# Four parts of the modulation rows as running sums on VectorE, started beside the retention heads

## The chip, the cores and the metric

One core of one Trainium2 chip runs the whole kernel in one launch. The metric is the device time of a run in microseconds. The engines of the core each follow a queue of their own, in order: TensorE (PE, with its weight loads PEld), VectorE (DVE), ScalarE (ACT), GpSimd (POOL) and SyncE (SP), which issues most loads. They meet through semaphores only.

## What is computed

Two transformer blocks on 512 tokens of width 1024, with 256 tokens of context. Each block begins with a modulation, whose six rows of 1024 numbers scale, shift and gate the block's two branches:

```python
def _modulation(cvec, w, b, n):
    m = jax.nn.silu(cvec) @ w[:, : n * D_MODEL] + b[: n * D_MODEL]
    return jnp.split(m, n, axis=-1)

sh1, sc1, g1, sh2, sc2, g2 = [m[:, None, :] for m in _modulation(c, w_mod[i], b_mod[i], 6)]
cm = _modulation(c_ctx, w_mod[i], b_mod[i], 2 if last else 6)
...
hx = _rmsnorm(x, norm_mix_pre[i]) * (1.0 + sc1) + sh1
...
x = x + g1 * _rmsnorm(_mixer_out(ret_x, gdn_x, rg, gz, gates, *out_p), norm_mix_post[i])
h2 = _rmsnorm(x, norm_ffn_pre[i]) * (1.0 + sc2) + sh2
x = x + g2 * _rmsnorm(_moe(h2, *moe_p), norm_ffn_post[i])
```

A vector of 1024 goes through a matrix of 1024 x 6144 float32 numbers (25 MB), once in each block (`w_mod`, `w_mod_2`). The first two rows (`sh1`, `sc1`) are needed for the context vector too. The first block mixes by a gated delta net (gdn) and by retention, two heads of each in either direction, then runs a mixture of 64 experts; the second block mixes by a convolution and neighbourhood attention and runs 16 experts. The outputs of both mixers go through `w_gdn_out` and `w_ret_out`, then `w_o`.

## The kernel before

A modulation is computed in three parts of 2048 columns (`bk` 0 to 2, two rows each). Part 0 of `w_mod` comes first, before anything else can run; five parts are later ones. `mod_part` (lines 300 to 322) loads eight tiles of 128 x 2048 (1 MB each), one ahead of use, and multiplies each by the 32-column tile `cm` of the activated vectors, in four products that stand side by side in the array's four groups of 32 columns:

```python
for g in range(4):
    nc.tensor.matmul(ps[32 * g:32 * g + 32, :], cm[:, k, :], wt[:, g * 512:(g + 1) * 512],
                     start=(k == 0), stop=(k == ND - 1), tile_position=(0, 32 * g))
for _ in range(pause):
    yield
```

Then ScalarE copies the sums to `brow` (line 313), PE transposes them (line 228), and VectorE adds the bias into `mcol` (line 321). `mod_part` is a generator: `self.start` puts it on the list `chains`, and `tick`, which `dense` calls after every few products (line 253), moves each generator on by one `yield`. So ticks decide where between the large products the later parts are recorded, and that is the order of every engine's queue.

Before, `later_mods` starts at the head of the first mixer. It lays out the constants of retention (`ret_consts`), then the five parts with a pause of two ticks per tile, so all five lie beside the gdn heads, from 59 to 308 us of the span.

All tiles of large matrices (`w_mod`, `w_in`, `w_gdn_out`, `w_ret_out`, `w_o`, later the experts) come out of one pool of `NW` = 4 buffers, through `wload` (line 176) on SyncE's queue, in the order in which they are recorded. A load waits until a buffer's last reader is done. In most weights each tile is split into a high and a low half: a cast on ScalarE (line 211) and a subtraction on POOL or VectorE (line 212), and the product is three products of halves (line 253).

`mix_out` (lines 1140 to 1171) holds four buffers at once, two of `w_gdn_out` and two of `w_ret_out`. It takes the gdn side first (`br` = 1), then the retention side (`br` = 0), and before that side's splits it empties the list of generators:

```python
raw = [[self.wrows(n, 256 * i, 2) for i in range(2)] for n in ("w_gdn_out", "w_ret_out")]
for br in (1, 0):
    if br == 0:
        self.rows1 = self.mix_rows()
    while self.yT[br][0] is None or self.yT[br][1] is None or (br == 0 and self.chains):
        self.tick()
```

`mix_rows` needs rows of `w_mod`; the rows of `w_mod_2` are needed only in the second block.

Of the kernel before, what the change touches and what calls it, by code (L numbers as in the profile page):

```python
# [16 lines left out]
OP = mybir.AluOpType  # L17
# [4 lines left out]
P = 128  # L22
D = 1024
ND = 8
# [74 lines left out]
AHEAD, EARLY = 2, (2, 2, 3, 3)  # L99
W1, W2, W4, W5 = 5.5, 1.8, 6.0, 3.0  # L100
TAPS = 16

LOADS2, ORDER2 = 12, "vvvvbb"

# [14 lines left out]
class K:  # L119
# [180 lines left out]
    def mod_part(self, w, b, cm, mcol, bk, pause):  # L300
# [19 lines left out]
        for r in range(2):  # L320
            nc.vector.tensor_add(dst[:, :, :, r], pt.rearrange("p j (g q) -> p g j q", g=4)[:, :, :, r],
                                 self.bcol[:, 48 * b + 16 * bk:48 * b + 16 * bk + 16].rearrange("p (g j) -> p g j", g=4))

    def bcast_row(self, cols, name):

        nc = self.nc
        dst = self.u(D, name=name)
        for h in range(2):
            ps = self.ps(4, P)
            self.transposes(ps, [cols[:, 4 * h + k:4 * h + k + 1].to_broadcast([P, P]) for k in range(4)])  # L330
            nc.scalar.copy(dst[:, h * 512:(h + 1) * 512], ps.rearrange("p a b -> p (a b)"))
        return dst
# [77 lines left out]
    def phase_a(self):  # L410
        nc, a, cp = self.nc, self.a, self.cp
        self.setup()
        self.w_in1()
        xt = [self.u(D, name="xt") for _ in range(4)]
        ct = [self.u(D, name="ct") for _ in range(2)]
        for t in range(2):
            nc.scalar.dma_start(ct[t], a["ctx"][t * P:(t + 1) * P])
        for t in range(4):
            nc.scalar.dma_start(xt[t], a["x"][t * P:(t + 1) * P])
        cm = self.silu_cols(R_C, "1")  # L420
        mcol = self.mcol = cp.tile([P, 48, 2], F32, name="mcol1")
        hc, hx = [], []
        self.start(self.rows_T(ct, hc, "hc", 5), self.rows_T(xt, hx, "hx", 4))
        for i, _ in enumerate(self.mod_part("w_mod", 0, cm, mcol, 0, 3)):
            if i in (10, 11):
                self.w_fetch(i - 10)
            if i in (22, 23):
                for _ in self.w_split(i - 22, 0):
                    pass
            self.tick()  # L430
        self.drain()
        gm = self.col[:, R_GMIX:R_GMIX + 8]
        Ax = self.mod_cols(gm, mcol, 1, 0, "x1")
        Ac = self.mod_cols(gm, mcol, 1, 1, "c1")
        self.hx = self.split_T(hx, 2, Ax, mcol[:, 0:8, 0], "hx", nc.vector)
        self.hc = self.split_T(hc, 4, Ac, mcol[:, 0:8, 1], "hc", nc.gpsimd)
        del hx, hc
        self.ghalf = cp.tile([P, 8], F32, name="ghalf")
        nc.vector.tensor_scalar(self.ghalf, self.col[:, R_RGN:R_RGN + 8], 0.5, None, op0=OP.mult)
        self.yT = [[None, None], [None, None]]  # L440
        self.gsp = self.dp.tile([16, P, NX], F32, name="gsp")
        self.start(self.later_mods(cm))
        self.gates_ab()
        gs = [SimpleNamespace(p=p, k=0, v=0, q=0, z=[]) for p in range(2)]
        for g in gs:
            self.gdn_feats(g)
            self.start(self.gdn_chain(g))
            for i in range(8):
                self.gate_spill(8 * g.p + i)
            self.out_gate(g)  # L450
        rs = [SimpleNamespace(p=p, z=[]) for p in range(2)]
        for r in rs:
            self.ret_feats(r)
            self.start(self.ret_chain(r))
            self.out_gate(r)
        self.mT = self.mix_out()

    def later_mods(self, cm):
        nc = self.nc
        yield from self.ret_consts()  # L460
        for bk in (1, 2):
            yield from self.mod_part("w_mod", 0, cm, self.mcol, bk, 2)
        cm2 = self.silu_cols(R_C2, "2")
        mcol = self.mcol2 = self.cp.tile([P, 48, 2], F32, name="mcol2")
        for bk in range(3):
            yield from self.mod_part("w_mod_2", 1, cm2, mcol, bk, 2)

    def w_stream(self, name, tiles, ahead):

# [1393 lines left out]
    def phase_c(self):  # L1863
# [3 lines left out]
        ys, taps = self.conv_mixer(h)  # L1867
        qkv, rest = self.attn_proj(h, itertools.islice(taps, TAPS))
        self.attention(qkv, rest, itertools.chain(taps, self.conv_tail(ys)))
# [529 lines left out]
```

## Times and profile before

| | |
|---|---|
| runs shown | 2811.13, 2811.26 and 2801.1 us, median 2811.13 |
| the profiled run's own time | 2811.13 us |
| its span | 2809.2 us |
| granted clock of TensorE, mean | 0.954 |
| PE busy | 2486.5 us, 89% |
| VectorE, ScalarE, POOL busy | 1056.1, 515.1, 541.5 us |

The span runs from the first to the last profiled instruction, and the run's own time is 1.9 us longer. Busy time is a sum over stages: in the gdn stage (59 to 308 us) TensorE is hardly ever idle, and in the second half of the kernel the loads of experts run nearly without pause. A row of the timeline gives start, duration, line, operation, tiles, count, and in brackets the idle time ahead with what ended it.

### The profile page before, as it was taken

How to read it: one execution, taken by the hardware profiler on the slowest of the kernel's cores; microseconds unless marked ns; L12 is line 12 of the kernel's file. 1: busy time of each engine (PE TensorE's matmuls, PEld its weight loads, DVE VectorE, ACT ScalarE, POOL GpSimd, SP SyncE). 2: the span in 40 equal slices, each digit the busy share in tenths (PEclk: the TensorE clock that was granted, in tenths of full speed). 3: DMA queues.
4: the chain of work that ended last, by engine and by line, in shares of the span. 5: the costliest groups of instructions: out<-in, count | busy, mean ns of one | idle time of the engine just before them, and what ended most of it. 6: DMA issues, size and time to landing. Idle time of an engine off the chain costs nothing.

```text
span 2809.2 us, 34992 instructions
## 1 busy us (share of the span) xinstructions
PE 2486.5 (89%) x13409; PEld 1373.5 (49%) x13409; DVE 1056.1 (38%) x2675; ACT 515.1 (18%) x1088; POOL 541.5 (19%) x392
## 2 busy tenths in 40 slices
PE   6999989999799998987895969968999899988887
PEld 3767869887454543433344857533333333333322
DVE  3573763454733532222323777231211212112213
ACT  4442532222211110100112225110000000000001
POOL 3152243334312221222233450000000000000000
PEclk8999999999899999999897989989999999999999
DMA  7576221134479999999996122259999999999996
GB/s 266 215 271 217 94 87 46 61 117 158 158 256 336 337 335 346 345 346 319 329 330 210 32 79 81 117 242 422 426 427 426 427 427 427 427 427 426 427 427 291
DMA packets 160154, 782.13 MB, mean 278 GB/s; under 512 B 20787, under 2 KB 66035, under 8 KB 121075
## 3 DMA queue, kind: packets, MB, share of 16 engines
q1 hardware_dynamic: 131504, 714.65, 65.2%
q0 software_dynamic: 16288, 37.79, 5.7%
q10 hardware_dynamic: 12194, 27.45, 2.7%
q8 instruction: 107, 1.75, 0.3%
q14 instruction: 61, 0.49, 0.1%
HBM read 752.73 MB, written 33.23 MB: 280 GB/s over the span
## 4 chain that ended last, share of the span: by engine, by line
PE 67%; DMA 17%; DVE 11%; issue 2%; ACT 2%; POOL 2%; SPq 0%; DVEq 0%; ACTq 0%; POOLq 0%
PE ps L253 17%; PE ps L2265 13%; PE ps L2284 8%; DMA wu<-in_w_expert 6%; PE ps L1638 6%; DMA w<-in_w_expert 6%; PE ps L228 5%; PE ps L224 4%; DMA wd<-in_w_expert 3%; PE ps L2213 2%; PE ps L2296 2%; PE ps L1635 2%; PE ps L309 2%; POOL wsl L212 1%; PE ps L1668 1%
## 5 line engine op out<-in xcount | busy, mean ns | idle before, releaser
L2265 PE MATMUL ps<-w,xT 128*64 128x512 f32 x2048 | 444.8, 593 | 7.5 <-DMA w<-in_w_expert 5.9
L2265 PEld LDWEIGHTS ps<-w,xT 128*64 128x64 f32 x2048 | 146.8, 137 | 302.9 <-issue 277.2
L2284 PE MATMUL ps<-w,hT 128*64 128x512 f32 x1024 | 229.6, 607 | 18.7 <-ACT hT L2276 18.7
L212 POOL TENSOR_TENSOR wsl<-w,wsh 128x1024 fp32r<-128x1024 f32 x60 | 174.5, 2917 | 259.8 <-ACT wsh L211 193.8
L2320 POOL TENSOR_TENSOR fin<-fin,norm_final_g 128x512 f32<-128x512 f32 x2 | 2.6, 1306 | 1105.1 <-ACT fin L2313 1105.1
L2271 DVE TENSOR_TENSOR hid<-hid,ps 128x512 f32<-128x512 f32 x32 | 22.0, 687 | 405.7 <-PE ps L2265 405.7
L1638 PE MATMUL ps<-w,xT 128*128 128x512 f32 (+6 forms) x320 | 149.5, 610 | 19.3 <-DMA w<-in_w_expert 11.4
L224 PE MATMUL ps<-wd,ehT 128*128 128x512 f32 (+6 forms) x320 | 150.8, 615 | 15.5 <-DVE eh L1649 12.4
L2284 PEld LDWEIGHTS ps<-w,hT 128*64 128x64 f32 x1024 | 73.3, 140 | 166.4 <-issue 141.5
L1638 PE MATMUL ps<-wu,xT 128*128 128x512 f32 (+6 forms) x320 | 147.2, 599 | 2.0 <-DMA wu<-in_w_expert 2.0
L1604 POOL DMA_INDIRECT xg<-h2d,sidx x65 | 67.0, 1031 | 329.5 <-PE ps L1668 169.0
L1659 DVE COPY ehT<-ps 128x256 f32<-128x256 f32 (+6 forms) x69 | 22.8, 330 | 277.0 <-PE ps L228 277.0
L1648 ACT ACTIVATE eh<-ps 128x256 f32<-128x256 f32 (+6 forms) x69 | 23.2, 337 | 497.6 <-PE ps L1638 313.7
L2270 ACT ACTIVATE hid<-ps 128x512 f32<-128x512 f32 x32 | 19.1, 597 | 512.3 <-PE ps L2265 512.3
L2289 DVE TENSOR_TENSOR y<-ps,G 128x512 f32<-128x512 f32 x16 | 11.1, 691 | 268.3 <-PE ps L2284 268.3
L1638 PEld LDWEIGHTS ps<-w,xT 128*128 128x128 f32 (+6 forms) x320 | 52.8, 169 | 107.1 <-issue 98.1
L1901 DVE SCALAR_TENSOR_TENSOR cy<-cv,cw,cy 128x512 f32<-128x512 f32 x120 | 101.6, 904 | 0.4
L253 PE MATMUL ps<-hxh,wsh 128*128 128x512 f32 x296 | 88.6, 428 | 5.5 <-ACT wsh L211 3.1
L224 PEld LDWEIGHTS ps<-wd,ehT 128*128 128x128 f32 (+6 forms) x320 | 51.5, 171 | 85.0 <-issue 57.2
L1638 PEld LDWEIGHTS ps<-wu,xT 128*128 128x128 f32 (+6 forms) x320 | 50.2, 165 | 73.3 <-issue 67.8
L2299 DVE TENSOR_TENSOR xr<-xr,ps 128x512 f32<-128x512 f32 x128 | 78.1, 680 | 19.4 <-PE ps L2296 19.4
L253 PE MATMUL ps<-hxh,wsl 128*128 128x512 f32 x296 | 83.9, 416 | 0.0
(644 smaller groups left out, 4166.0 us busy)
## 6 DMA issues: line engine op xcount, KB each, us to landing
w<-in_w_expert SPq DMA_DIRECT2D x191, 2048.0 KB, 17.5
w<-in_w_expert SPq DMA_DIRECT2D x64, 1024.0 KB, 15.6
wu<-in_w_expert SPq DMA_DIRECT2D x128, 512.0 KB, 15.8
wd<-in_w_expert SPq DMA_DIRECT2D x128, 512.0 KB, 13.8
w<-in_w_mod SPq DMA_DIRECT2D x48, 1024.0 KB, 5.6
w<-in_w_in SPq DMA_DIRECT2D x34, 1024.0 KB, 5.6
wa<-in_w_in SPq DMA_DIRECT2D x9, 512.0 KB, 9.6
gsp<-gsp POOLq DMA_DIRECT2D x16, 256.0 KB, 3.0
```

What stands on the lines that cost most here:

```text
L212: (lo or self.nc.vector).tensor_sub(low, x, hi.bitcast(F32))
L224: self.nc.tensor.matmul(ps, l, r, start=(i == 0), stop=(i == n - 1))
L228: self.nc.tensor.transpose(ps[:, i], s, self.ident[:parts, :parts])
L253: self.nc.tensor.matmul(ps, l, r, start=(i == 0), stop=(i == n - 1))
L309: nc.tensor.matmul(ps[32 * g:32 * g + 32, :], cm[:, k, :], wt[:, g * 512:(g + 1) * 512], start=(k == 0), stop=(k == ND - 1), tile_position ...
L1604: self.nc.gpsimd.indirect_dma_start(out=self.xg[b % 4][:c], out_offset=None, in_=self.h2d, in_offset=bass.IndirectOffsetOnAxis(ap=idx[:c], ...
L1635: nc.tensor.matmul(ps[64 * j:64 * j + 64, 0:256], x, w[k][:, 256 * j:256 * j + 256], start=first, stop=last, tile_position=(0, 64 * j))
L1638: nc.tensor.matmul(ps[:m], x, w[k], start=first, stop=last)
L1901: nc.vector.scalar_tensor_tensor(y[:, j], vs[j][:, k:k + NX], tap, y[:, j], op0=OP.mult, op1=OP.add)
L2265: nc.tensor.matmul(pgu[gi][c][64 * j:64 * j + 64], xT[:, k], w[2 * j + c], start=(k == 0), stop=(k == ND - 1), tile_position=(0, 64 * j))
L2284: nc.tensor.matmul(py[64 * j:64 * j + 64], hT[fc][:, ff, 64 * fj:64 * fj + 64], w[2 * r + j], start=(ft == 0), stop=(ft == 15), tile_posit ...
L2299: nc.vector.tensor_add(xh, xh, ps)
```

## The change

A new method `mod_row` computes a part for the first vector alone, with VectorE in place of the large products. Two running sums `macc` of 128 x 1024 take tile after tile: the first is a multiplication by a column of `cm` (line 336 after the change), the other seven a multiplication and addition in one instruction (line 338). After the eighth tile four products with a tile of ones (line 343) sum over the 128 partitions, and copy, transposes and one addition follow as before. The pause is `MODS` = 3 ticks after each half tile. Parts 1 and 2 of both matrices go this way; part 0 of `w_mod_2` stays with `mod_part`, comes last, and pauses six ticks per tile.

`later_mods` starts after the loop over the gdn heads, and the constants of retention, until now its first step, start by themselves where it stood. Lines after the new method move by 32, those before it by 1.

```diff
--- before.py
+++ after.py
@@ -99,6 +99,7 @@
 AHEAD, EARLY = 2, (2, 2, 3, 3)
 W1, W2, W4, W5 = 5.5, 1.8, 6.0, 3.0
 TAPS = 16
+MODS = 3

 LOADS2, ORDER2 = 12, "vvvvbb"

@@ -320,6 +321,37 @@
         for r in range(2):
             nc.vector.tensor_add(dst[:, :, :, r], pt.rearrange("p j (g q) -> p g j q", g=4)[:, :, :, r],
                                  self.bcol[:, 48 * b + 16 * bk:48 * b + 16 * bk + 16].rearrange("p (g j) -> p g j", g=4))
+
+    def mod_row(self, w, b, cm, mcol, bk, pause):
+
+
+        nc = self.nc
+        load = lambda k: self.wload(self.a[w][k * P:(k + 1) * P, bk * 2048:(bk + 1) * 2048])
+        acc, nxt = [self.u(D, name="macc") for _ in range(2)], load(0)
+        for k in range(ND):
+            wt, nxt = nxt, load(k + 1) if k + 1 < ND else None
+            for h in range(2):
+                v = wt[:, h * D:(h + 1) * D]
+                if k == 0:
+                    nc.vector.tensor_scalar(acc[h], v, cm[:, k, 0:1], None, op0=OP.mult)
+                else:
+                    nc.vector.scalar_tensor_tensor(acc[h], v, cm[:, k, 0:1], acc[h], op0=OP.mult, op1=OP.add)
+                for _ in range(pause):
+                    yield
+        ps, brow = self.ps(), self.u(512, name="brow")
+        for g in range(4):
+            nc.tensor.matmul(ps[32 * g:32 * g + 32], self.ones[:, 0:32], acc[g // 2][:, g % 2 * 512:g % 2 * 512 + 512],
+                             start=True, stop=True, tile_position=(0, 32 * g))
+        yield
+        nc.scalar.copy(brow, ps)
+        yield
+        yield
+        pt = self.ps(4, P)
+        self.transposes(pt, [brow[:, j * P:(j + 1) * P] for j in range(4)])
+        yield
+        dst = mcol.rearrange("p (b g j) r -> p b g j r", b=3, g=4)[:, bk, :, :, 0]
+        nc.vector.tensor_add(dst, pt.rearrange("p j (g q) -> p g j q", g=4)[:, :, :, 0],
+                             self.bcol[:, 48 * b + 16 * bk:48 * b + 16 * bk + 16].rearrange("p (g j) -> p g j", g=4))

     def bcast_row(self, cols, name):

@@ -439,7 +471,7 @@
         nc.vector.tensor_scalar(self.ghalf, self.col[:, R_RGN:R_RGN + 8], 0.5, None, op0=OP.mult)
         self.yT = [[None, None], [None, None]]
         self.gsp = self.dp.tile([16, P, NX], F32, name="gsp")
-        self.start(self.later_mods(cm))
+        self.start(self.ret_consts())
         self.gates_ab()
         gs = [SimpleNamespace(p=p, k=0, v=0, q=0, z=[]) for p in range(2)]
         for g in gs:
@@ -448,6 +480,7 @@
             for i in range(8):
                 self.gate_spill(8 * g.p + i)
             self.out_gate(g)
+        self.start(self.later_mods(cm))
         rs = [SimpleNamespace(p=p, z=[]) for p in range(2)]
         for r in rs:
             self.ret_feats(r)
@@ -456,14 +489,13 @@
         self.mT = self.mix_out()

     def later_mods(self, cm):
-        nc = self.nc
-        yield from self.ret_consts()
         for bk in (1, 2):
-            yield from self.mod_part("w_mod", 0, cm, self.mcol, bk, 2)
+            yield from self.mod_row("w_mod", 0, cm, self.mcol, bk, MODS)
         cm2 = self.silu_cols(R_C2, "2")
         mcol = self.mcol2 = self.cp.tile([P, 48, 2], F32, name="mcol2")
-        for bk in range(3):
-            yield from self.mod_part("w_mod_2", 1, cm2, mcol, bk, 2)
+        for bk in (1, 2):
+            yield from self.mod_row("w_mod_2", 1, cm2, mcol, bk, MODS)
+        yield from self.mod_part("w_mod_2", 1, cm2, mcol, 0, 2 * MODS)

     def w_stream(self, name, tiles, ahead):

```

What this does to three queues at the place where the two sides of `mix_out` meet follows.

SyncE's queue issues the loads. Before, two loads of `w_in` and the mixers' output matrices stand ahead of the four loads of `w_o`:

```order
L176 DMA w_5375<-in_w_in 128x8x256
L176 DMA w_5621<-in_w_in 128x8x256
L176 DMA w_5889<-in_w_gdn_out 128x2x1024
L176 DMA w_5891<-in_w_gdn_out 128x2x1024
L176 DMA w_5893<-in_w_ret_out 128x2x1024
L176 DMA w_5895<-in_w_ret_out 128x2x1024
L176 DMA w_6301<-in_w_o 128x2x1024
L176 DMA w_6303<-in_w_o 128x2x1024
L176 DMA w_6305<-in_w_o 128x2x1024
L176 DMA w_6307<-in_w_o 128x2x1024
```

After, the series of loads that follows `w_gdn_out` is:

```order
L177 DMA w_5662<-in_w_gdn_out 128x2x1024
L177 DMA w_5664<-in_w_gdn_out 128x2x1024
L177 DMA w_5666<-in_w_ret_out 128x2x1024
L177 DMA w_5668<-in_w_ret_out 128x2x1024
L177 DMA w_5718<-in_w_mod 128x2048
L177 DMA w_5783<-in_w_mod 128x2048
L177 DMA w_6023<-in_w_mod 128x2048
L177 DMA w_6025<-in_w_mod 128x2048
L177 DMA w_6072<-in_w_mod 128x2048
L177 DMA w_6076<-in_w_mod 128x2048
L177 DMA w_6080<-in_w_mod 128x2048
L177 DMA w_6084<-in_w_mod 128x2048
```

The two loads `w_5718` and `w_5783` are the last of `w_mod`; behind them stand 24 loads of `w_mod_2`, then `w_o`, then the experts. Before, all 40 later loads of the modulation stand between loads of `w_in`, far ahead of this place.

On VectorE before, the retention head's last steps (`ro`, `yT`) are followed by the splits of the retention side (`yml`) and the gated sum of its first product (`gt`):

```order
L205 SCALAR_TENSOR_TENSOR rs_6175<-rqc_6185,rs_6175 128x8
L1136 TENSOR_SCALAR ro_5829<-ro_5829,bmv_6144,rs_6175 128x128 x8
L880 SCALAR_TENSOR_TENSOR yT_6217<-ps_6218,ghalf,gz_5764 128x512
L880 SCALAR_TENSOR_TENSOR yT_6217<-ps_6241,ghalf,gz_5764 128x512
L212 TENSOR_TENSOR yml_1284_6261<-yT_5636,ymh_1283_6260 128x1024
L212 TENSOR_TENSOR yml_1290_6273<-yT_6217,ymh_1289_6272 128x1024
L1163 SCALAR_TENSOR_TENSOR gt_6284<-gt_6284,ps_6286 128x512
```

After, behind the new column sums `cm` for the second block, the running sums stand between and behind them (`w_6023` is the first tile of `w_mod_2`):

```order
L297 TENSOR_TENSOR cm_1243_6013<-col,sce_6015 128x8x2
L392 SCALAR_TENSOR_TENSOR Af_6036<-mcol_106,col 128x8
L336 TENSOR_SCALAR macc_6021<-w_6023,cm_1243_6013 128x1024
L912 SCALAR_TENSOR_TENSOR yT_6028<-ps_6029,ghalf,gz_5532 128x512
L338 SCALAR_TENSOR_TENSOR macc_6021<-w_6025,cm_1243_6013,macc_6021 128x1024
L912 SCALAR_TENSOR_TENSOR yT_6028<-ps_6052,ghalf,gz_5532 128x512
L336 TENSOR_SCALAR macc_6022<-w_6023,cm_1243_6013 128x1024
L338 SCALAR_TENSOR_TENSOR macc_6022<-w_6025,cm_1243_6013,macc_6022 128x1024
L338 SCALAR_TENSOR_TENSOR macc_6021<-w_6072,cm_1243_6013,macc_6021 128x1024
L338 SCALAR_TENSOR_TENSOR macc_6022<-w_6072,cm_1243_6013,macc_6022 128x1024
L338 SCALAR_TENSOR_TENSOR macc_6021<-w_6076,cm_1243_6013,macc_6021 128x1024
```

All of part 1 and part 2 of `w_mod_2`, 32 instructions, stand there, ahead of the first gated sum.

On PE before, the transposes of the last rows stand directly ahead of the retention side's products (`ymh`, `wmh`):

```order
L228 MATMUL ps_6234<-cst,Af_6225 128x128 x4
L228 MATMUL ps_6218<-cst,ro_5829 128x128 x3
L228 MATMUL ps_6241<-cst,ro_5829 128x128
L228 MATMUL ps_6247<-cst,mcol_106 128x128 x4
L228 MATMUL ps_6253<-cst,mcol_106 128x128 x4
L228 MATMUL ps_6241<-cst,ro_5829 128x128 x3
L253 MATMUL ps_6286<-ymh_1283_6260,wmh_1285_6264 128x512
L253 MATMUL ps_6311<-ymh_1283_6260,wmh_1285_6264 128x512
L253 MATMUL ps_6332<-ymh_1283_6260,wmh_1285_6264 128x512
```

After, the end of part 2 of `w_mod_2` and the whole of its part 0 stand ahead of the first of those products:

```order
L343 MATMUL ps_6145<-macc_6112,cst 32x512 x2
L229 MATMUL ps_6152<-cst,brow_6146 128x128 x4
L310 MATMUL ps_6159<-w_6160,cm_1243_6013 32x512 x4
L310 MATMUL ps_6159<-w_6162,cm_1243_6013 32x512 x4
L310 MATMUL ps_6159<-w_6168,cm_1243_6013 32x512 x4
L310 MATMUL ps_6159<-w_6174,cm_1243_6013 32x512 x4
L310 MATMUL ps_6159<-w_6180,cm_1243_6013 32x512 x4
L310 MATMUL ps_6159<-w_6186,cm_1243_6013 32x512 x4
L310 MATMUL ps_6159<-w_6192,cm_1243_6013 32x512 x4
L310 MATMUL ps_6159<-w_6198,cm_1243_6013 32x512 x4
L229 MATMUL ps_6209<-cst,brow_6158 128x128 x4
L254 MATMUL ps_6242<-ymh_1291_6216,wmh_1293_6220 128x512
```

Eight groups of four products (line 310), each on a tile that is loaded there, have moved from the gdn stage to this place.

## Rows read from the trace of the kernel before

**Rows 1.** The page, part 1: engine, busy us (share of the span), instructions.

```profile
PE 2486.5 (89%) x13409; PEld 1373.5 (49%) x13409; DVE 1056.1 (38%) x2675; ACT 515.1 (18%) x1088; POOL 541.5 (19%) x392
```

**Rows 2.** PE by line and form: name, shape, count, busy us, mean ns.

```profile
L309 PE MATMUL ps<-w,cm 128*32 128x512 f32 x384 | 59.5, 631 | 2.8 <-DVE cm L296 2.4 <-DMA w<-in_w_mod 0.4
```

**Rows 3.** Windows of line 309 alone: stretch, PE busy (count), weight loads, clock, DMA, GB/s.

```profile
59.00:158.50 99.50, 20.79 (x128) 3.24 (x128) 0.97 0.60 212
...
158.50:203.00 44.50, 10.35 (x72) 1.65 (x72) 1.00 0.77 266
...
203.00:308.00 105.00, 18.13 (x124) 2.62 (x120) 1.00 0.61 209
```

**Rows 4.** Timeline of POOL near 73 us: start, duration, line, operation.

```profile
72.72 2.40 POOL L388 TENSOR_TENSOR hcl<-hc,hch 128x1024 fp32r<-128x1024 f32 x1
```

**Rows 5.** Timeline of PE near 77 and near 203 us.

```profile
77.00 0.63 PE L253 MATMUL ps<-hcl,wsh 128*128 128x256 f32 x4
...
203.00 0.31 PE L944 MATMUL ps<-Tc,Lc 32*32 32x32 f32 x8
```

**Rows 6.** Windows, all engines (PE, weight loads, DVE, ACT, POOL; clock, DMA, GB/s).

```profile
98.33:122.87 24.54, 24.02 (x159) 16.36 (x158) 22.00 (x77) 11.55 (x41) 3.97 (x2) 1.00 0.51 181
...
158.50:201.10 42.60, 42.60 (x229) 27.74 (x228) 39.41 (x96) 12.81 (x26) 11.92 (x13) 1.00 0.80 276
...
203.00:308.00 105.00, 105.00 (x917) 76.37 (x914) 40.11 (x129) 38.53 (x101) 31.68 (x34) 1.00 0.61 209
...
500.00:600.00 100.00, 95.75 (x670) 89.64 (x669) 48.39 (x155) 26.30 (x43) 37.96 (x21) 0.97 0.27 96
```

**Rows 7.** Timeline of DVE, end of the first inverse.

```profile
196.84 2.28 DVE L919 STREAM_TRANSPOSE Tc<-T 128x1024 f32<-128x1024 f32 x1
```

**Rows 8.** DVE by line and form, a multiplication and addition on 128x1024.

```profile
L1464 DVE SCALAR_TENSOR_TENSOR mix<-xr,rs,Ar 128x1024 f32<-128x1024 f32 x2 | 2.5, 1272 | 0.0
```

**Rows 9.** Timelines of POOL and DVE near 562 us.

```profile
562.31 2.81 POOL L212 TENSOR_TENSOR wml<-w,wmh 128x1024 fp32r<-128x1024 f32 x1 [11.90 <-ACT wmh L211]
...
559.19 0.29 DVE L1084 TENSOR_SCALAR vw<-rVc,rw 128x128 f32<-128x128 f32 x1 [0.70 <-ACT rVc L1060]
...
562.79 2.82 DVE L1084 TENSOR_SCALAR vw<-rVc,rw 128x128 f32<-128x128 f32 x3
```

**Rows 10.** Timelines of DVE and PE, end of the last retention head, output products.

```profile
628.45 0.75 DVE L880 SCALAR_TENSOR_TENSOR yT<-ps,ghalf,gz 128x512 f32<-128x512 f32 x1 [0.26 <-PE ps L228]
...
630.76 7.41 PE L253 MATMUL ps<-ymh,wmh 128*128 128x512 f32 x25 [2.34 <-ACT wmh L211]
...
659.81 5.49 PE L253 MATMUL ps<-wqh,mph 128*128 128x512 f32 x23
```

**Rows 11.** The page, part 6: loads, count, KB, median us from issue to landing.

```profile
w<-in_w_mod SPq DMA_DIRECT2D x48, 1024.0 KB, 5.6
...
w<-in_w_gdn_out SPq DMA_DIRECT2D x2, 1024.0 KB, 4.8
```

**Rows 12.** The page, part 2: GB/s moved in 40 equal slices of the span.

```profile
GB/s 266 215 271 217 94 87 46 61 117 158 158 256 336 337 335 346 345 346 319 329 330 210 32 79 81 117 242 422 426 427 426 427 427 427 427 427 426 427 427 291
```

**Rows 13.** Timeline of SyncE's DMA queue: first issue, length of the series, load, count.

```profile
520.99 10.86 SPq L176 DMA_DIRECT2D w<-in_w_gdn_out  x2
...
550.44 33.83 SPq L176 DMA_DIRECT2D w<-in_w_ret_out  x2
...
589.65 58.01 SPq L176 DMA_DIRECT2D w<-in_w_o  x4
```

**Rows 14.** POOL by line and form, 600 to 680 us.

```profile
L212 POOL TENSOR_TENSOR wql<-w,wqh 128x1024 fp32r<-128x1024 f32 x7 | 20.2, 2908 | 9.2 <-DVE mpl L212 9.2
```

**Rows 15.** Timeline of PE after the second inverse, 384 to 404 us.

```profile
393.01 1.06 PE L944 MATMUL ps<-Tc,Lc 32*32 32x32 f32 x32 [8.16 <-DVE Tc L919]
...
394.00 3.78 PE L253 MATMUL ps<-hxh,wsl 128*128 128x512 f32 x8
...
397.58 2.39 PE L253 MATMUL ps<-hxl,wsh 128*128 128x512 f32 x8
```

## The prediction

> **What bounds the kernel now.** I read the page first: PE is busy for 2486.5 of 2809.2 us [rows 1], so work taken off PE is worth time wherever PE itself is the limit. Whether it is can only be read by stage. The list of PE's instructions by line gives the disputed work: line 309 has 384 records, 59.5 us [rows 2], 320 of them in the five later parts. The windows place these: 20.8, 10.35 and 18.1 us of PE time in three stretches from 59 to 308 us, 49.3 in all [rows 3], or 1.23 us for each of 40 tiles. The timelines of POOL, PE and VectorE then show where PE follows another engine [rows 4 to 7], and last I read the place where the two sides of the mixer's output meet, at 628 us, on VectorE, PE and the load queue [rows 10, 13]. The granted clock is 0.97 to 1.00 in the three stretches [rows 3], so PE there runs at its upper level.
>
> **What is removed: PE work in the gdn stage.** 49.3 us is the most that can come back. It will not all come, because PE meets other engines:
>
> - Until 158.5 us, 20.8 us go. But POOL finishes `hcl` at 72.72 + 2.40 = 75.12 and PE takes it at 77.00 [rows 4, 5], so up to there PE can gain 1.9 at most; and from 98.3 to 122.9 VectorE is busy for 22.0 of 24.5 us [rows 6], which leaves 2.5. Low end 1.9 + 2.5 = 4.4, high end 20.8; I take 8.9, nearer to the low end since both meetings lie in this stretch.
> - From 158.5 to 203, 10.35 go, beside the inverse on VectorE, which is busy for 39.4 of 42.6 us [rows 6]. Its last transposition ends at 196.84 + 2.28 = 199.12 [rows 7] and PE takes it at 203.00 [rows 5]: no more than 3.9 can be gained. I take 3.9.
> - From 203 to 308, 18.1 go. PE is busy for 105 of 105 us, the others for under 41 [rows 6]. I keep 85%, 15.4, for some splits that will be late.
>
> Sum: 28 us earlier (low end 15, high end 49).
>
> **What is added beside the retention heads.** The first two running rows (parts 1 and 2 of `w_mod`) are 2 x 16 instructions of 128x1024. The nearest row is a multiplication and addition of that shape at 1.27 us [rows 8]: 40.7 us of VectorE. VectorE is busy for 48.4 of 100 us there [rows 6], so they fit; but the queue is in order, and a sum whose tile has not landed holds up what stands behind it (the rope, the decays, the states), for which PE waits. On PE each row adds four products with ones; a tile of line 309, also four, costs 1.23, so 2.5 us, and with eight transposes 3, on a PE that is busy for 95.75 of 100. Low end 3, high end 3 + 41, if every sum delays PE; I take 8, near the low end because half of VectorE is free. The constants of retention start where they did: nothing.
>
> The sums also meet POOL's splits. Three small VectorE instructions that began at 562.79, inside a POOL split from 562.31 to 565.12, took 2.82 us, until 565.61 [rows 9]. The Trainium skill ("SBUF — State Buffer", section "SBUF: two separate sides") says that VectorE and GpSimd share one pair of ports, as an exclusive lock which the loser waits for, also for a VectorE instruction with two inputs in SBUF against a GpSimd one that reads SBUF. The trace agrees in these 2.82 us; what it would cost here is the third rival.
>
> **What is moved to the place where the sides meet.** This is the term that decides. SyncE's order has 24 loads of `w_mod_2` behind the output matrices, VectorE's has all 32 running sums of its two rows ahead of the retention side's first gated sum, and PE's has the last part, line 310, ahead of that side's first product. Nothing of this can run ahead: `w_gdn_out`'s buffers pass to the last two tiles of `w_mod` and then to the first two of `w_mod_2`, while `w_ret_out` holds the other two until the retention side is split. So from 628.5 on [rows 10] 22 tiles of 1 MB must be loaded, used and dropped before PE may go on, with little else to do.
>
> - A tile's round in its buffer is load, two sums, and a step to the next load. A single load of this size takes 4.8 us [rows 11] (5.6 where others run beside it), the sums 2 x 1.27, the steps some 0.2 as an estimate: 7.6 us. Two buffers in turn give 3.8 us for a tile.
> - The first ten tiles go at that pace, 38 us. The copy of the first row lets ScalarE and POOL split the first tile of `w_ret_out`, and a third buffer comes free. Then 7.6 / 3 = 2.5, about the peak rate: 1.05 MB at 427 GB/s [rows 12] are 2.46 us. With 2.6 for a tile the other twelve take 31. The last eight are used by PE, at 1.23.
> - Filling ahead of the first load is 2.5, landing and use of the last tile with its copy and transposes another 3.
>
> 38 + 31 + 5.5 = 74.5 from 628.5, so 703; copy and transposes reach 704.5. Today that product starts at 630.76 [rows 10]: 74 us later. Low end: 22 tiles at the peak rate, 54 - 2 = 52. High end: two buffers all through with loads of 5.6, 22 x 4.2 less 2, 90.
>
> Here row and page differ. The row has 4.8 to 5.6 us for 1 MB [rows 11]. The Trainium skill ("DMA: Bandwidth & Descriptors", section "Measured") gives 6.15 us for such a transfer. By the page the first ten tiles would take 4.4 each as an estimate, and the gap would be about 80 instead of 74. I go by the row.
>
> Two small things follow. After an idle time of 8.16 us PE's next eight products took 3.78 us and the eight after them 2.39 [rows 15]; such a slow start after the gap is +2. And `w_o`, loaded today from 589.65 on [rows 13], comes behind all tiles. Three of its loads go out as the last tiles are read, some 3 us ahead of the products; landing 5 and eight splits on POOL of 2.9 [rows 14] end 25 us into them, and they are needed after 659.81 - 630.76 = 29 [rows 10]. Hidden with 4 us to spare; if that cover is gone, up to 6.
>
> **Sum.** Against the profiled run's own time, 2811.1, which is also the median: -28 + 8 + 74 + 2 = +56, so 2867 us. All low ends together give -49 + 3 + 52 = +6, all high ends -15 + 44 + 90 + 2 + 6 = +127.
>
> **The rivals.**
>
> 1. The gdn stage gives back all of 49 us. For it: PE is full in all three stretches [rows 3, 6]. Against: the 1.9 and 3.9 us of margin [rows 4, 5, 7]. -49 + 8 + 74 + 2 = +35, 2846 us. Chance 0.20.
> 2. No gap: the loads and sums of `w_mod_2` run beside the retention side's products, as `mod_part` does beside large products today. Then -28 + 8 = -20, 2791 us, faster. It decides from the point where the gap is under 20 us. For it: nothing in the second row's result is needed before the second block. Against: the order on three engines, and two buffers. Chance 0.04.
> 3. The sums and POOL exclude each other beside the retention heads. POOL is busy for 38.0 of 100 us there and VectorE for 48.4 [rows 6]; with 40.7 more that is 127 in a stretch of 100 to 130, and VectorE sets the pace. It adds about 30: 2897 us. The skill's page named above is where this rule stands. The one overlap seen [rows 9] speaks for it, the short share of such overlaps against. Chance 0.16.
> 4. The gap is near its low end of 52 and the gdn stage gives most back: +5 to +14, 2820 us, about no change. Chance 0.03.
>
> The forecast itself has 0.57. Its own range is 2852 to 2884, from the gap's pace of 2.5 to 4.2 us per tile and the gdn stage's 20 to 36. To hold 8 in 10 I reach from 2832, half way between the first rival and the fourth, to the third rival, 2896. The time of this kernel is told from no change at about 0.5%, 14 us. Faster by more: 0.04; within: 0.03; slower: 0.93.
>
> **What would show it.** In the profile after: line 310 and the sums of `w_mod_2` in one stretch of about 75 us with PE nearly idle, waiting for loads of `w_mod`, between the last retention head and the retention side's products; issues of `w_mod` 3.8 us apart at first and some 2.6 later; PE reaching the first inverse's result about 13 us sooner and the end of the gdn stage 28 sooner; waits for VectorE of a few us among the retention heads. The forecast is wrong if the gap is under 45 us, if the gdn stage ends less than 15 us sooner, or if PE's waits ahead of the gap grow by over 20.

## The result, and the profile after

The changed kernel takes 2897.59 us (median of four runs, 2895.13 to 2899.31), the kernel before 2807.93 beside it: a ratio of 1.032, interval 1.030 to 1.0341. It is slower by 90 us. The prediction had the direction and the place, and 2867; its range ended at 2896, 1.6 us short of the time.

The two profiled executions differ by 86.1 us of span. Five places on PE, read from its timeline (start of the first record, us), say where this arises:

| place on PE | before | after | shift |
|---|---|---|---|
| the first inverse is taken up (`Tc,Lc`) | 203.00 | 194.11 | -8.9 |
| the second inverse is taken up | 393.01 | 374.26 | -18.8 |
| last products of the retention states (`vw,rKx`) | 611.17 | 617.05 | +5.9 |
| first product of the retention side (`ymh,wmh`) | 630.76 | 716.44 | +85.7 |
| end of the span | 2809.2 | 2895.3 | +86.1 |

The rows of the middle two places (PE's timeline merges equal products into one row, so a place is good to 1 us):

```profile
374.26 0.96 PE L976 MATMUL ps<-Tc,Lc 32*32 32x32 f32 x28 [8.14 <-DVE Tc L951]
...
617.05 0.38 PE L1123 MATMUL ps<-vw,rKx 128*128 128x128 f32 x2
```

Before, the second inverse is taken up as in [rows 15], and the last states follow at:

```profile
611.17 1.27 PE L1091 MATMUL ps<-vw,rKx 128*128 128x128 f32 x10
```

So three terms, each in its own stage: 18.8 us of relief in the gdn stage, a loss of 24.6 beside the retention heads, a gap of 79.8 ahead of the retention side. From there on nothing more is lost.

PE's busy time has hardly changed (the page, part 1, against [rows 1]):

```profile
PE 2474.7 (85%) x13185; PEld 1385.8 (48%) x13185; DVE 1140.0 (39%) x2735; ACT 514.6 (18%) x1088; POOL 546.6 (19%) x392
```

The gap, in a window over all engines (columns as in [rows 6]): PE is busy for 18.6 of 82.4 us, at a mean granted clock of 0.62 against 1.00 in the 17 us ahead of it; VectorE is busy for half of the time, and the loads run at 303 GB/s.

```profile
634.00:716.40 82.40, 18.59 (x92) 3.81 (x93) 42.69 (x37) 7.53 (x9) 8.03 (x3) 0.62 0.83 303
```

**The gdn stage**, in PE's timeline. PE takes `hcl` at 74.96, two us sooner [rows 5], and then meets VectorE again and again where tiles of line 309 used to lie: 4.12 us for `gK`, 3.37 for the inverse, 5.22 for the second head's `gK`.

```profile
74.96 2.08 PE L254 MATMUL ps<-hcl,wsh 128*128 128x256 f32 x8 [6.25 <-POOL hcl L420]
...
117.48 1.45 PE L229 MATMUL ps<-cst,gK 128*128 128x128 f32 x6 [4.12 <-DVE gK L682]
...
194.11 0.69 PE L976 MATMUL ps<-Tc,Lc 32*32 32x32 f32 x32 [3.37 <-DVE Tc L951]
...
265.60 1.54 PE L229 MATMUL ps<-cst,gK 128*128 128x128 f32 x6 [5.22 <-DVE gK L682]
```

**The retention heads**, from the second inverse to the last states, in windows over all engines. Before, 118 and 101 us:

```profile
393.00:511.00 118.00, 113.91 (x1053) 104.51 (x1054) 42.68 (x126) 35.99 (x91) 44.97 (x44) 0.95 0.19 59
...
511.00:612.00 101.00, 100.83 (x705) 93.86 (x705) 50.05 (x171) 23.67 (x40) 35.62 (x20) 1.00 0.31 105
```

After, 125 and 117 us, with VectorE busy for 18 and 21 us more. Over both stretches PE stands idle for 21 us where it was 4, and is busy for 6 longer; its granted clock in the second is 0.94, not 1.00:

```profile
375.00:500.00 125.00, 114.52 (x1033) 103.52 (x1029) 60.93 (x142) 34.97 (x89) 50.12 (x42) 0.96 0.35 114
...
500.00:617.00 117.00, 106.34 (x720) 97.57 (x719) 70.90 (x190) 24.45 (x41) 35.45 (x21) 0.94 0.43 154
```

How a sum gets in the way is seen on VectorE near 460 us: two sums, held 0.53 us by their tile's load and then 2.48 long, stand ahead of the scan's `vp`.

```profile
459.35 2.48 DVE L338 SCALAR_TENSOR_TENSOR macc<-w,cm,macc 128x1024 f32<-128x1024 f32 x2 [0.53 <-DMA w<-in_w_mod]
...
461.83 0.61 DVE L842 SCALAR_TENSOR_TENSOR vp<-ps,neg,gV 128x128 f32<-128x128 f32 x2
```

PE waits for that `vp` (1.22 us), and at 565 us for the normalised output `ro` (9.89), which in the kernel before it had after 1.1:

```profile
463.01 1.21 PE L254 MATMUL ps<-wsh,hch 128*128 128x256 f32 x8 [1.22 <-DVE vp L842]
...
565.31 1.47 PE L229 MATMUL ps<-cst,ro 128*128 128x128 f32 x5 [9.89 <-DVE ro L1168]
```

This one wait is the largest piece of the loss. Six sums, 7.7 us, stand on VectorE between the first step of that normalisation (543.78) and its last (564.82). And three of its small steps, beside two splits and a small product on POOL, took 5.1 us together (2.19, 0.65 and 2.26):

```profile
558.61 2.19 DVE L198 TENSOR_TENSOR rqu<-rs 128x8 f32<-128x8 f32 x1
...
561.51 2.26 DVE L200 SCALAR_TENSOR_TENSOR rs<-rqu,rs 128x8 f32<-128x8 f32 x1
```

```profile
558.39 2.38 POOL L213 TENSOR_TENSOR wml<-w,wmh 128x1024 fp32r<-128x1024 f32 x1 [10.49 <-ACT wmh L212]
...
561.41 2.34 POOL L213 TENSOR_TENSOR wsl<-w,wsh 128x1024 fp32r<-128x1024 f32 x1
```

In the kernel before, with POOL idle, each of the three took 0.17:

```profile
557.11 0.17 DVE L197 TENSOR_TENSOR rqu<-rs 128x8 f32<-128x8 f32 x1
```

**The gap.** On VectorE the sums of `w_mod_2` come in pairs, each pair behind the landing of its tile, 3.73 us apart in the mean (640.19 to 658.85 are five steps). Then a third buffer comes free, and the first two sums that meet POOL's splits take 6.24 in place of 2.48:

```profile
640.19 2.48 DVE L338 SCALAR_TENSOR_TENSOR macc<-w,cm,macc 128x1024 f32<-128x1024 f32 x2 [3.49 <-DMA w<-in_w_mod]
...
643.94 2.48 DVE L338 SCALAR_TENSOR_TENSOR macc<-w,cm,macc 128x1024 f32<-128x1024 f32 x2 [1.27 <-DMA w<-in_w_mod]
...
658.85 2.48 DVE L338 SCALAR_TENSOR_TENSOR macc<-w,cm,macc 128x1024 f32<-128x1024 f32 x2 [1.09 <-DMA w<-in_w_mod]
...
666.48 6.24 DVE L338 SCALAR_TENSOR_TENSOR macc<-w,cm,macc 128x1024 f32<-128x1024 f32 x2 [0.25 <-DMA w<-in_w_mod]
```

POOL's splits at that place:

```profile
665.96 5.68 POOL L213 TENSOR_TENSOR wml<-w,wmh 128x1024 fp32r<-128x1024 f32 x2 [32.99 <-issue]
```

PE does three small pieces in between, the sums over partitions of both rows (`macc`, the second at 690.78) and line 310, and then begins the products of [rows 10]:

```profile
660.19 3.12 PE L343 MATMUL ps<-macc,cst 128*32 128x512 f32 x8 [27.59 <-DVE macc L338]
...
710.52 1.06 PE L310 MATMUL ps<-w,cm 128*32 128x512 f32 x8 [3.33 <-DMA w<-in_w_mod]
...
716.44 2.05 PE L254 MATMUL ps<-ymh,wmh 128*128 128x512 f32 x4
```

SyncE's queue issues the 26 loads from 593.54 on over 112 us, and `w_o` behind them, where it began at 589.65 before [rows 13]:

```profile
593.54 112.05 SPq L177 DMA_DIRECT2D w<-in_w_mod  x26
...
707.26 27.10 SPq L177 DMA_DIRECT2D w<-in_w_o  x4
```

### The profile page after: what moved, and what is told of

It reads as the page before. It is cut to its first block, busy times and chain, and to the rows that moved or that the text cites. A ratio compares the mean times of both kernels' runs of the same rounds, so it can differ in the third digit from the quotient of the medians.

```text
span 2895.3 us, 34608 instructions
## 1 busy us (share of the span) xinstructions
PE 2474.7 (85%) x13185; PEld 1385.8 (48%) x13185; DVE 1140.0 (39%) x2735; ACT 514.6 (18%) x1088; POOL 546.6 (19%) x392
## 4 chain that ended last, share of the span: by engine, by line
PE 59%; DMA 19%; DVE 14%; issue 3%; ACT 2%; POOL 2%; SPq 0%; DVEq 0%; ACTq 0%; POOLq 0%
PE ps L2297 14%; PE ps L254 13%; PE ps L2316 8%; DMA wu<-in_w_expert 6%; PE ps L1670 5%; PE ps L229 5%; DMA w<-in_w_expert 4%; PE ps L225 4%; DMA w<-in_w_mod 3%; DMA wd<-in_w_expert 3%; PE ps L2245 2%; PE ps L2328 2%; DMA acb<-ey,sidx 2%; DVE macc L338 1%; PE ps L1667 1%
## 5 line engine op out<-in xcount | busy, mean ns | idle before, releaser
L225 PE MATMUL ps<-wd,ehT 128*128 128x512 f32 (+6 forms) x320 | 150.1, 613 | 13.5 <-DVE eh L1681 9.4
L338 DVE SCALAR_TENSOR_TENSOR macc<-w,cm,macc 128x1024 f32<-128x1024 f32 x56 | 77.4, 1418 | 26.5 <-DMA w<-in_w_mod 26.3
```

The lines of the kernel that those rows point to most:

```text
L225: self.nc.tensor.matmul(ps, l, r, start=(i == 0), stop=(i == n - 1))
L338: nc.vector.scalar_tensor_tensor(acc[h], v, cm[:, k, 0:1], acc[h], op0=OP.mult, op1=OP.add)
```

## The experiments

Each kernel was timed beside the kernel before (medians of 2807.5 to 2808.9 us). Two stretches of PE's timeline in each profile are read with the total: A, from the second inverse to the last products of the retention states, and B, from there to the first product of the retention side.

| kernel | median us | ratio, interval | A | B |
|---|---|---|---|---|
| before | 2808 | | 218.2 | 19.6 |
| after | 2897.6 | 1.032, 1.030 to 1.0341 | 242.8 | 99.4 |
| e1_no_mod2 | 2816.0 | 1.002, 1.0002 to 1.0037 | 243.4 | 22.3 |
| e2_no_late | 2780.3 | 0.9899, 0.9869 to 0.993 | 217.4 | 21.6 |
| e3_parts_late | 2837.4 | 1.0099, 1.0068 to 1.0131 | 269.2 | 19.0 |
| e4_rows_early | 2855.0 | 1.0164, 1.0132 to 1.0195 | 238.3 | 18.8 |
| e5_mods1 | 2860.7 | 1.0184, 1.0165 to 1.0203 | 285.0 | 24.1 |
| e7_ret_later | 2870.9 | 1.0227, 1.021 to 1.0244 | 241.0 | 80.1 |
| e8_one_tile | 2837.1 | 1.0111, 1.0091 to 1.0132 | 237.2 | 21.6 |
| e9_short | 2817.8 | 1.0035, 1.002 to 1.005 | 248.9 | 18.3 |
| e10_half_gap | 2883.1 | 1.0271, 1.0254 to 1.0289 | 247.0 | 89.4 |
| e11_half_ret | 2797.5 | 0.9959, 0.9945 to 0.9973 | 223.5 | 23.2 |
| b_pause3 | 2807.7 | 0.9995, 0.9983 to 1.0006 | 218.9 | 19.6 |
| b_pause4 | 2798.5 | 0.9965, 0.9954 to 0.9976 | 221.8 | 20.2 |

Three of them (e2, e8, e11) give the first block other rows, so its tokens go to other experts, and what follows is another amount of work: from their totals nothing is concluded, only from A and B, which lie ahead of it. A repeats to some 5 us (`after`, e1, e7 and e10 have the same sums there and 241 to 247).

**The gap alone.** `later_mods` ends behind the two rows of `w_mod`:

```diff
-        for bk in (1, 2):
-            yield from self.mod_row("w_mod_2", 1, cm2, mcol, bk, MODS)
-        yield from self.mod_part("w_mod_2", 1, cm2, mcol, 0, 2 * MODS)
...
+        self.nc.vector.tensor_copy(self.mcol2[:, :, 0], self.mcol[:, :, 0])
...
```

> The changed kernel without the three parts of w_mod_2 (left out: their 24 loads, sums and products; the second block takes the first block's rows). Theory A, three separate terms: the gdn stage comes 19 us sooner, the retention stage loses 24 us to the running sums, and the emptying of the list ahead of the retention side costs 81. Then only the third term goes: 2897.6 - 81 = 2817 us (2811 to 2823), with nothing between the last retention head and that side's products. Rival B, the gap hides other work (w_o's loads, splits) that is late in any case: no more than half of it comes back, 2855 or above.

2815.96 us, as theory A has it: 82 us go with the 24 tiles, 77.1 of them at B, and rival B is out. PE's timeline has the last states and the next side's first product 22.3 us apart:

```profile
617.68 0.38 PE L1121 MATMUL ps<-vw,rKx 128*128 128x128 f32 x2
...
639.93 1.51 PE L254 MATMUL ps<-ymh,wmh 128*128 128x512 f32 x3 [2.62 <-ACT wmh L212]
```

**No later part at all.** The two rows of `w_mod` are replaced by copies as well.

> The changed kernel without any of the five later parts (left out: all their loads, sums and products; both blocks take the first rows' columns). Theory A: the 24 us lost from 374 to 617 us are the running sums' and their loads', so they go too: 2817 - 24 = 2793 us (2786 to 2799), which is before less the 19 us of relief; PE then does not wait 9.9 us for the normalised retention output. Rival C, the loss in that stage comes from the other order of the queues after the move and not from the sums: it stays, 2812 to 2820.

At the places that count theory A holds: A is 217.4, within a microsecond of before. Its PE timeline:

```profile
372.85 1.06 PE L976 MATMUL ps<-Tc,Lc 32*32 32x32 f32 x32 [8.16 <-DVE Tc L951]
...
590.22 1.27 PE L1123 MATMUL ps<-vw,rKx 128*128 128x128 f32 x10
```

This fixes both other terms. All 49 us of PE work are gone, and PE comes to the second inverse 20.2 us sooner, no more; up to there it stands idle for 27 us more than before, so the rest had filled waits. And the 25.4 us by which A is longer in the changed kernel belong to the two rows of `w_mod`. The total of 2780 is 13 below the expectation, behind these places.

**Products at the new place.** `mod_part` with a pause of 2 in place of `mod_row` and of the last line.

> The changed kernel with the products of before (mod_part, pause of 2 ticks) in place of the running sums, at the new place beside the retention heads. In its order five loads of w_mod_2 are left behind the output matrices, not 24. Theory A, the gap goes with the number of tiles left over: it is 10 to 16 us; the 40 tiles' 49 us of PE now lie where PE is full; VectorE's stall goes. 2808 - 19 + 49 + 12 = 2850 us (2838 to 2860). Rival D, VectorE's sums are the whole loss and the place is harmless: 2805 to 2815.

2837.4, just under the range, and outside D. A is 51 us longer than before, which is the products' 49 us on a full PE; but B is 19.0: five loads left over cost nothing, where I had 10 to 16. PE's timeline:

```profile
645.31 1.05 PE L1122 MATMUL ps<-vw,rKx 128*128 128x128 f32 x4
...
664.32 1.88 PE L254 MATMUL ps<-ymh,wmh 128*128 128x512 f32 x7 [2.27 <-ACT wmh L212]
```

**Sums beside the gdn heads.** The start of `later_mods` goes back to its old place:

```diff
-        self.start(self.ret_consts())
+        self.start(self.ret_consts(), self.later_mods(cm))
...
-        self.start(self.later_mods(cm))
```

> The changed kernel with the later parts started where before starts them, beside the gdn heads, sums on VectorE and pace as in the change. Three loads are left behind the output matrices. Theory A: gap 8 us at most; PE has 34 us less to do; the sums that fall into VectorE's own chains (98 to 123, 158 to 203, 310 to 375 us, about a quarter of the 81 us of sums) cost about 20. 2808 - 20 + 20 = 2808 us (2792 to 2825). Rival D, sums on VectorE stall PE by about 0.75 us each wherever they stand: 64 x 0.75 = 48, 2808 - 34 + 48 + 8 = 2830 or above.

2855.0: theory A's size was wrong and rival D right. PE takes the first inverse up at 217.47, 14.5 us later than before and 24 later than without the sums. Its waits from 59 to 640 us (waiting line, awaited, us, times, longest), 25.5 for the inverses and 18.3 for `go`, were 8.2 and 5.4 before:

```profile
PE ps L975 <- DVE Tc L950: 25.5, 2, 16.3
...
PE ps L229 <- DVE go L809: 18.3, 2, 11.6
```

The retention side's first product comes at 671.10, 59 us later than in e2. With some 10 of them for the last part's products, that is about 0.8 us for each of the 64 sums, as beside the retention heads (25 us for 32). So the late place is not the only cause of the loss.

**A closer pace.**

```diff
-MODS = 3
+MODS = 1
```

> The changed kernel with MODS = 1, so that the sums follow each other three times as closely and eight loads, not 24 of w_mod_2, are left behind the output matrices. Theory A (gap by tiles left over, each sum beside the heads costs 0.85 us): relief -20, 64 sums +54, last part's eight tiles on PE +10, gap 10: 2808 + 54 = 2862 us (2850 to 2872); the last retention head ends some 40 us later than before. Rival E, the 24 loads cost 80 us wherever they stand, since the load queue has no room for them: 2885 or above.

2860.7, theory A's number. B is 24.1 with eight tiles left over, A 285.0 with the 64 sums and the last part in it: the pace turns the gap into a stall, a third smaller. PE's longest waits from 375 to 690 us are for `ro`:

```profile
PE ps L229 <- DVE ro L1168: 23.9, 3, 18.9
```

**More buffers for the gap.**

```diff
-        raw = [[self.wrows(n, 256 * i, 2) for i in range(2)] for n in ("w_gdn_out", "w_ret_out")]
+        raw = [[self.wrows("w_gdn_out", 256 * i, 2) for i in range(2)]]
...
+            if br == 0:
+                raw.append([self.wrows("w_ret_out", 256 * i, 2) for i in range(2)])
```

> The changed kernel with the two loads of w_ret_out recorded behind the emptying of the list, so that the 22 tiles in the gap have four buffers and not two or three; the retention side's weights then land and are split only after it. Theory A, buffers set the gap's pace: 2.6 us for a tile from the first on (the sums' 2.5 and the peak rate's 2.46 are next), 57 in place of 82, and 10 us for the late weights: 2897.6 - 15 = 2882 us (2872 to 2890). Rival F, the loads' rate or the sums set the pace already: no gain, and the late weights on top, 2903 to 2908.

2870.9, just under theory A's range, and rival F is out. B is 19.3 us shorter, and the sums run in long series, 1.25 us each:

```profile
642.99 8.76 DVE L338 SCALAR_TENSOR_TENSOR macc<-w,cm,macc 128x1024 f32<-128x1024 f32 x7 [0.85 <-DMA w<-in_w_mod]
```

The late weights cost PE 7.62 us inside the products:

```profile
694.33 3.92 PE L254 MATMUL ps<-ymh,wmh 128*128 128x512 f32 x16 [1.27 <-ACT wmh L212]
...
705.87 4.21 PE L254 MATMUL ps<-ymh,wmh 128*128 128x512 f32 x9 [7.62 <-ACT wmh L212]
```

From the first product of the experts' stage to the end, its profile is 13.5 us shorter than the changed kernel's, which I can't explain from this change. So its total overstates what the buffers gave, and the 19.3 of B is the measure.

**No reloading.** As e1, with one tile for each row:

```diff
-        acc, nxt = [self.u(D, name="macc") for _ in range(2)], load(0)
+        acc, wt = [self.u(D, name="macc") for _ in range(2)], load(0)
...
-            wt, nxt = nxt, load(k + 1) if k + 1 < ND else None
```

> As e1_no_mod2 (w_mod_2 left out), and each of the two rows of w_mod sums its first tile eight times, so that 14 loads are left out and no sum waits for one; the 32 sums stay where they are. e1_no_mod2 took 2816.0 and e2_no_late, without sums, was 27 us ahead of it at the last retention state. Theory G, VectorE's queue is held by sums whose tile has not landed (13 us of such waits in the changed kernel): 2803 us (2799 to 2807). Rival H, it is the 40 us of the sums themselves: 2813 to 2819.

The total says nothing here. A is 237.2 with 32 sums that wait for no load (last states at 610.06), so G's 13 us are not there; 6 us may be the loads', within the repeat of A.

```profile
610.06 1.17 PE L1120 MATMUL ps<-vw,rKx 128*128 128x128 f32 x9
```

**Shorter sums.** As e1, with `for h in range(4)` on 512 columns each and `for _ in range(2 - h % 2)` ticks.

> As e1_no_mod2 (w_mod_2 left out), with each tile of the two rows of w_mod summed in four instructions of 128x512 and not two of 128x1024, a pause of 2, 1, 2, 1 ticks after them; the same six ticks per tile. e1_no_mod2 took 2816.0, of which its 32 sums cost 27 us at the last retention state. Theory I, each sum is a delay put into the exchange between PE and VectorE, as long as the one instruction that stands ahead: half as long a piece delays half as much, though twice as often, and more of them fall into VectorE's idle times: 2806 us (2802 to 2811). Rival J, the sums' total time counts, with 0.06 us more for each of 32 further instructions: 2815 to 2821.

2817.8 and A 248.9: rival J. Halving the length of one instruction gains nothing.

**Half of the sums in the gap.**

```diff
-                if k == 0:
+                if b and h:
+                    pass
+                elif k == 0:
```

> The changed kernel with only the first half of each tile of w_mod_2's two rows summed (16 of their 32 sums left out, the second half takes the first one's sums); all loads and ticks as in the change. Theory A, a tile's round in its buffer sets the pace: (4.9 + 1.27 + 0.2) / 2 = 3.2 in place of 3.8 us while two buffers serve, little after that, so 6 to 9 us less: 2890 us (2886 to 2893). Rival F, VectorE's sums set it: 16 x 1.27 = 20 us less, 2877 or below. Rival, the loads' rate alone sets it: 2895 to 2899.

2883.1, between A and F; B is 10 us shorter. Of the total's 14.5, 9 lie in the experts' stage, as unexplained as in e7, so B alone is read. VectorE's timeline shows that A's price of the first steps is right and that it missed a part behind them: a step is 3.2 us in the mean on two buffers (641.86 to 657.83 are five), but then 2.49 for a tile, the loads' own rate, which the sums' 2.5 had just covered in the changed kernel:

```profile
641.86 1.28 DVE L340 SCALAR_TENSOR_TENSOR macc<-w,cm,macc 128x1024 f32<-128x1024 f32 x1 [1.17 <-DMA w<-in_w_mod]
...
645.17 1.28 DVE L340 SCALAR_TENSOR_TENSOR macc<-w,cm,macc 128x1024 f32<-128x1024 f32 x1 [2.03 <-DMA w<-in_w_mod]
...
657.83 1.28 DVE L340 SCALAR_TENSOR_TENSOR macc<-w,cm,macc 128x1024 f32<-128x1024 f32 x1 [2.00 <-DMA w<-in_w_mod]
...
680.66 1.28 DVE L340 SCALAR_TENSOR_TENSOR macc<-w,cm,macc 128x1024 f32<-128x1024 f32 x1 [1.21 <-DMA w<-in_w_mod]
...
683.15 1.28 DVE L340 SCALAR_TENSOR_TENSOR macc<-w,cm,macc 128x1024 f32<-128x1024 f32 x1 [1.21 <-DMA w<-in_w_mod]
```

**Half of the sums beside the heads.** As e1, with `if h: pass` in the same place for both rows.

> As e1_no_mod2 (w_mod_2 left out), with only the first half of each tile of w_mod's two rows summed (16 of the 32 sums left out); all 16 loads and all ticks as there. From the second inverse to the last retention state e1_no_mod2 takes 243.4 us, e2_no_late without sums or loads 217.4. The first block's rows change with it, so its experts' load changes too, and it is read at that place and not by its end. Theory K, the cost goes with VectorE's time taken: half of it, 217.4 + 13 = 230 us (227 to 233). Rival L, it goes with the loads that share SyncE's queue and the buffers: 240 us or above.

A is 223.5, 6 us over the kernel without any, where K had 13 and L 23 or more:

```profile
376.58 1.06 PE L976 MATMUL ps<-Tc,Lc 32*32 32x32 f32 x32 [7.32 <-DVE Tc L951]
...
600.09 1.28 PE L1123 MATMUL ps<-vw,rKx 128*128 128x128 f32 x10
```

All loads are there, and VectorE stands for 24.4 us ahead of sums that wait for them, twice as long as in e1 (VectorE's list by line, 395 to 625 us: count, busy us, mean ns, idle time ahead). In e11:

```profile
L340 DVE SCALAR_TENSOR_TENSOR macc<-w,cm,macc 128x1024 f32<-128x1024 f32 x14 | 21.3, 1520 | 24.4 <-DMA w<-in_w_mod 24.4
```

In e1:

```profile
L338 DVE SCALAR_TENSOR_TENSOR macc<-w,cm,macc 128x1024 f32<-128x1024 f32 x28 | 39.6, 1443 | 12.2 <-DMA w<-in_w_mod 12.0
```

So it is not the waiting for loads that costs. 16 sums cost 6 us, 32 cost 20 (e8) to 26 (e1). Most of that step is one place, PE's wait for the normalised `ro` of the changed kernel's 565 us. It lasts 9.5 to 11.7 us in all six kernels with 32 sums there (`after`, e1, e7, e8, e9, e10), 0.9 in e11, and PE has no such wait in e2. In PE's waits over A, e1 and then e11:

```profile
PE ps L229 <- DVE ro L1166: 9.6, 1, 9.6
...
PE ps L229 <- DVE ro L1168: 0.9, 1, 0.9
```

In e11 one sum, not six, stands inside that normalisation, and POOL's split comes behind its small steps, none of which takes more than 0.17 us. No run takes those six sums away alone, so the shares of the sums and of POOL in this wait are read from traces and not shown by an edit. With A repeating to 5 us, what is left over does not tell whether the cost grows faster than the number of sums.

**Products, spread further.** The kernel before, with pauses of three and four ticks in place of two.

> The kernel before, all five parts as products beside the gdn heads, with a pause of three ticks per tile and not two, so that they reach past the second head's features, where PE waits for VectorE (1.6, 8.2 us in the kernel before; 5.2 for gK in the changed one). Theory A, a part's products are free where PE would wait: 2808 - 6 = 2802 us (2797 to 2805). Rival: those waits belong to VectorE's chain, which the later end of the first stretch moves along: 2806 to 2811.

2807.7, no difference that can be told, so the rival's case and not theory A's.

> The kernel before with a pause of four ticks per tile: the five parts as products reach from the gdn heads to about 500 us. b_pause3 took 2807.7 and gained 2 us up to the second inverse. If the tiles that now lie behind the second inverse meet a full PE there, nothing more comes back: 2806 to 2812 us. If they fill waits for the retention constants and the last scan: 2798 to 2804, which would be ahead of both kernels.

2798.5, 0.35% less than before (0.24 to 0.46%), and ahead of both kernels. Line 309 alone, in b_pause4 (columns as in [rows 3]): 17.7 us of it lie ahead of 203 us, 10.2 from there to 308, and 17.5 behind 308 us, up to 500.

```profile
59.00:203.00 144.00, 17.70 (x128) 3.16 (x128) 0.96 0.51 174
...
308.00:400.00 92.00, 8.11 (x64) 1.46 (x64) 0.94 0.49 170
...
400.00:500.00 100.00, 9.35 (x64) 1.49 (x64) 1.00 0.39 129
```

In its timeline PE takes up the inverses at 193.84 and 379.74, 9.2 and 13.3 us sooner than before (with no later part at all, e2, it is 9.4 and 20.2), and gives back 3.6 in A, though 9.35 us of tiles lie there. It needs no sum on VectorE, and no load left over for a gap.

## Why the prediction came out too low

| term of the sum | predicted | measured |
|---|---|---|
| relief in the gdn stage | -28 | -18.8 (e2: -20.2) |
| beside the retention heads | +8 | +24.6 (e2, e1: 25.4 to 26) |
| the gap, up to the next side's first product | +74 | +79.8 (e1: 77.1) |
| the slow start and all behind it | +2 | +0.4 |

- **The gap: right.** The place, two buffers in turn and the third one were as described, the pace 3.73 for the predicted 3.8. It was 5.8 us short, and the largest piece of that is POOL: its splits of `w_ret_out` ran beside the sums, and two sums took 6.24 us for 2.48. The Trainium skill ("SBUF — State Buffer", section "SBUF: two separate sides") has VectorE and GpSimd exclude each other there; the 3.76 us agree. The slow start is there too, a granted clock of 0.52 from 716.4 to 722 us and 2.05 us for four products that later take 1.07, but only 0.4 us is left of it at the end. The prediction set 6.15 us for 1 MB beside its row, from the Trainium skill ("DMA: Bandwidth & Descriptors", section "Measured"). That figure is for transfers that GpSimd issues. These are SyncE's, and a load and its steps took 5.0 us here, as the row had it.
- **The step that failed: the price of the sums beside the retention heads.** I had bounds of 3 and 44 us and chose 8, near the low end, since "half of VectorE is free". That is a share over 100 us and says nothing of when. PE needed VectorE's small steps at once, and 32 sums of 42 us cost 25: 17 us more of idle PE and 6 more of busy PE. The largest piece is the one wait of 9.9 us for `ro`. PE's waits before could not tell this, since before it stood idle for 4 us only in these stretches; the rows to read were VectorE's, the steps that lead to `ro` and what the new order puts between them.
- **The relief was the second miss, a third too high.** The reasoning up to the first inverse was right (`hcl`, the 3.9 us), and 12.8 became 8.9. From 203 to 308 I kept 85%, on the ground that PE is full and the others are not. But a full PE may be full because the tiles fill its waits: without them the second head's `gK` left it idle for 5.22 us. 9.9 of 18.1 came back.
- **The third rival** had the right place, and its 2897 us is the time measured. That is luck: it had VectorE set the pace, and VectorE was busy for 131.8 of 242 us there. The exclusion is in the trace, and matters in part: 28 of the sums took 1.37 us in the mean against 1.27 [rows 8], 3 us in all, and the three small steps ahead of `ro` took 4.6 us too long. The first rival, that all of the 49 comes back, is refuted by e2.
- **Three slips in the working.** No terms are given for the relief's low end of 15. The 5.5 us behind the tiles hold the last copy and transposes, and the step from 703 to 704.5 counts them again. And with a relief of 20 to 36 and the gap's 52 to 90, the forecast's own range would be 2837 to 2891, not 2852 to 2884.

With relief and stall as measured, the sum would have been -19 + 25 + 76 = +82.

## What to carry to other kernels

An engine that looks half idle is not a free place for work if the busy one waits for its answers: find the chains of small steps that the busy engine takes up at once, and count what the new order puts between their links. Here 32 sums of 42 us cost 25, and 10 of it was one wait behind such a chain. Work on a full engine is not worth its duration either, when it lies where that engine would wait; leaving it out altogether, as e2 does, measures what there is to gain before anything is moved. And before work is moved to a later place, count the tiles that the order leaves behind its last consumer, and the buffers that are free there.

## What the runs showed of the hardware

Loads of 1 MB, issued one after another from one queue, each into a buffer that had just come free, landed 2.49 us apart (e10, 421 GB/s). With two buffers in turn, a round less the sums leaves 5.0 us for a load and its steps in the changed kernel (7.5 - 2.5). In the gap PE, busy for 18.6 of 82.4 us, had a granted clock of 0.62 in the mean, and the products of line 310 there took up to 1.06 us where the fastest take 0.59. VectorE steps of 0.17 us took up to 2.26 beside a split on POOL of 2.34.
